# A new head for the first FFN: chunk by chunk, with shift and scale vectors computed as columns

## The chip, the cores and the metric

The kernel runs on one NeuronCore of a Trainium2 chip, in one launch. The metric is the device time of that launch in microseconds. Five engines work side by side, each through its own queue of instructions in order: TensorE (PE in the profile), VectorE (DVE), ScalarE (ACT), GpSimd (POOL) and SyncE (SP), which here issues nearly all DMAs. They wait for each other through semaphores. Weights stream from HBM into SBUF, PE multiplies into PSUM banks, and ACT, DVE and POOL work on what lies between.

## The reference, cut to what matters

Two layers over 256 tokens of width 1024, float32. Every layer is FFN, mixer, FFN; each of the three begins with an RMSNorm whose result is scaled and shifted by vectors that come from one condition vector c:

```python
cond = jax.nn.silu(c)                                  # c: (1, 1024)
for l in range(2):
    mod = cond @ ada_w[l] + ada_b[l]                   # ada_w[l]: (1024, 9 * 1024)
    (sh1, sc1, g1, sh2, sc2, g2, sh3, sc3, g3) = jnp.split(mod, 9, axis=-1)
    n1 = rmsnorm(h, norm_ffn1[l]) * (1 + sc1[:, None, :]) + sh1[:, None, :]
    h = h + 0.5 * g1[:, None, :] * swiglu(n1, ffn1_w_gu[l], ffn1_w_down[l])   # D_FF = 2816
    n2 = rmsnorm(h, norm_mix[l]) * (1 + sc2[:, None, :]) + sh2[:, None, :]
    h = h + g2[:, None, :] * hybrid_mixer(n2, ...)
    n3 = rmsnorm(h, norm_ffn2[l]) * (1 + sc3[:, None, :]) + sh3[:, None, :]
    h = h + 0.5 * g3[:, None, :] * swiglu(n3, ffn2_w_gu[l], ffn2_w_down[l])
return rmsnorm(h, final_norm)
```

swiglu multiplies by w_gu (1024 x 5632: gate and up halves), takes silu(gate) * up, and multiplies by w_down (2816 x 1024). Each of the nine vectors of a layer costs a product of cond with a 1024 x 1024 matrix, 4 MB of weights that are used once.

## The kernel before

**Operands.** Products keep nearly float32 precision with three passes: every operand is split into a rounded part "hi" and the rest "lo", and hi*hi, hi*lo and lo*hi are added in PSUM. `split` (L229) does it for weights: ACT copies a 128x1024 half of a loaded unit into hi (L236), DVE subtracts it from the raw data into lo (L237). Weights come in the order in which the kernel asks for them, packed by the host into one stream. `load` (L209) takes the next unit, mostly 1 MB (128 partitions x 2048 columns), into one of three "raw" buffers; six hi and six lo buffers follow. A buffer is loaded again when its last reader is done, so the SP queue runs ahead by three units at most.

**An FFN** (`ffn`, L645) has 11 blocks of 256 hidden columns. `get_gu` loads and splits a block's gate and up weights (2 MB); `gu_mm` multiplies with the weights as the stationary operand and the transposed activations `nT` as the moving one: 64 matmuls, 32 of 512 columns and 32 of 256. `gu_act` (L740) takes the result out of PSUM (ACT copies, DVE adds, ACT applies silu), POOL multiplies silu(gate) by up (L748), ACT rounds the product and POOL subtracts for the low part (L750). The down product of a block (`down`, L754) is 24 matmuls of 512 columns; it runs one block behind the gate/up product, and the last two blocks' run at the end, tile by tile. Block 0 is different: it is multiplied by rows (tokens on the output partitions, 512 columns), its product transposed on PE afterwards (`rows_act`).

**Shift, scale and gate vectors of later stages** are computed in jobs beside the FFN and mixer blocks, in the order of ADA_PLAN: beside the first FFN G1, SC2, SH2, SC3, SH3; beside the second FFN of layer 0 G3 and then SC1, SH1, SC2 of layer 1; beside the first FFN of layer 1 SH2, G1, SC3, SH3; gates alone elsewhere. One step (`Ada.step`, L406) loads two 128-row slices of the matrix, and DVE multiplies each by its element of cond and accumulates into a 128x1024 sum (L419, L421). After four steps `finish` (L428) adds over the partitions: for a shift or scale 8 transposes on PE (L445, through L194) and two reductions on DVE (L446), for a gate a product with ones. `Jobs.run` spreads the steps over JOB_PARTS blocks.

**The head** (`lead`, L680) works through the list LEAD. It loads the first scale (SC1) and shift (SH1) as row slices in two column spans, 0 to 767 and 768 to 1023. PE forms SC1 as rank-one products, cond element by element against the rows (L484); DVE accumulates SH1 (L489); `cols` (L491) turns both into columns by small matmuls. x is loaded, normalized and transposed meanwhile. With a span's columns there, ACT and DVE modulate and split (`modulate`, L684) and PE multiplies block 0 by rows. Loads that must not disturb are tied to others by `hold`.

**Order.** The program text gives every instruction a priority; a planner with its own timeline fixes the order of each engine's queue before launch, and `high_priority` lifts what is on a stage's edge (norms, gu_act, residuals). `after` adds an ordering by hand.

## Time and profile before

| | |
|---|---|
| median of the runs | 1102.63 us (3 runs, 1100.06 to 1104.28) |
| the profiled execution | 1099.71 us, its span 1097.9 us |
| PE busy | 1064.1 us, 97% |
| DVE busy | 814.3 us, 74% |
| ACT busy | 622.2 us, 57% |
| POOL busy | 219.1 us, 20% |
| DMA | 255.33 MB, 233 GB/s over the span |

Busy times come from one profiled execution. The profile also cuts the span into stretches of chosen length ("windows") with the busy time of each engine, the granted clock of PE as a share of full speed (PEclk) and the data moved; follows the chain of waits back from the last instruction; and lists single instructions by time (the timeline) or in groups by line and shape. PE's matmuls are pipelined, so their recorded durations overlap; the distance between starts is what a matmul costs in a full stream. On DVE the records of neighbours overlap a little as well. "POOL TENSOR_TENSOR" durations include any wait that happens inside the instruction.

### The profile page before, as it was taken

The numbers are of one execution on the slowest core, as the hardware profiler recorded it, in microseconds if no ns is written. First come the engines' busy times: TensorE is split into PE (matmuls) and PEld (weight loads), VectorE is DVE, ScalarE is ACT, GpSimd is POOL, SyncE is SP. The second block draws the span as 40 slices with busy tenths as digits, with TensorE's granted clock in tenths as the row PEclk, the third lists the DMA queues.
The fourth block names the chain that finished last, engine by engine and source line by source line (L and its number), as shares of the span: only waits on it lengthen the run. The fifth ranks groups of instructions, "written<-read, shape, count | busy, mean of one in ns | idle before, by whom it ended". The sixth has DMA issues, their size and how long they took to land.

```text
span 1097.9 us, 15773 instructions
## 1 busy us (share of the span) xinstructions
PE 1064.1 (97%) x5750; PEld 884.0 (81%) x5750; DVE 814.3 (74%) x1327; ACT 622.2 (57%) x1191; POOL 219.1 (20%) x223
## 2 busy tenths in 40 slices
PE   4999999999999999999999999999999999999997
PEld 1688888878888688888878888887788778888885
DVE  4688887877696687786889877886769757656663
ACT  2655454556766665455556554555676657555561
POOL 2022432411000022222311222231200001222221
PEclk9799999999999999999999999999999999999999
DMA  8878987945355187877848787883536515666551
GB/s 296 298 277 347 338 332 263 344 157 215 109 210 192 42 303 283 292 272 259 296 175 305 280 292 288 299 308 134 204 115 204 177 72 198 234 229 227 208 190 38
DMA packets 39997, 255.33 MB, mean 233 GB/s; under 512 B 4936, under 2 KB 5320, under 8 KB 12016
## 3 DMA queue, kind: packets, MB, share of 16 engines
q1 hardware_dynamic: 39168, 252.61, 63.5%
q0 software_dynamic: 752, 1.71, 0.5%
q8 instruction: 45, 0.74, 0.3%
q14 instruction: 32, 0.26, 0.1%
HBM read 253.24 MB, written 1.07 MB: 232 GB/s over the span
## 4 chain that ended last, share of the span: by engine, by line
PE 90%; ACT 3%; DMA 3%; DVE 2%; issue 1%; POOL 1%; SPq 0%; DVEq 0%; POOLq 0%; ACTq 0%
PE pb L189 49%; PE pa L189 38%; PE pb L194 3%; DMA raw<-in_stream_dram 2%; PE pa L194 1%; DVE acc L421 1%; ACT hi L236 1%; DVE lo L237 1%; DMA h<-in_x_dram 0%; ACT z L527 0%; ACT nT L569 0%; ACT z L569 0%; POOL ss L320 0%; POOL pr L748 0%; ACT qkB L1099 0%
## 5 line engine op out<-in xcount | busy, mean ns | idle before, releaser
L237 DVE TENSOR_TENSOR lo<-raw,hi 128x1024 fp32r<-128x1024 f32 (+3 forms) x314 | 381.0, 1229 | 141.7 <-ACT hi L236 139.8
L189 PE MATMUL pb<-nT,hi 128*128 128x512 f32 x1280 | 451.3, 394 | 0.0
L236 ACT CAST hi<-raw 128x1024 fp32r<-128x1024 f32 (+3 forms) x314 | 318.5, 1036 | 195.2 <-PE pb L189 87.6
L189 PE MATMUL pb<-nT,lo 128*128 128x256 f32 x1280 | 358.4, 282 | 0.0
L189 PEld LDWEIGHTS pb<-nT,hi 128*128 128x128 f32 x1280 | 239.2, 188 | 53.4
L189 PEld LDWEIGHTS pb<-nT,lo 128*128 128x128 f32 x1280 | 240.6, 188 | 3.4
L748 POOL TENSOR_TENSOR pr<-sil,pr 128x256 f32<-128x256 f32 x80 | 91.3, 1141 | 492.2 <-DVE pr L745 414.3
L421 DVE SCALAR_TENSOR_TENSOR acc<-raw,cond,acc 128x1024 f32<-128x1024 f32 x118 | 157.5, 1335 | 26.2 <-DMA raw<-in_stream_dram 23.1
L189 PE MATMUL pa<-hi,chh 128*128 128x512 f32 x336 | 106.8, 393 | 0.9 <-ACT chh L750 0.9
L189 PE MATMUL pa<-lo,chh 128*128 128x512 f32 x336 | 106.4, 391 | 0.0
L189 PE MATMUL pa<-hi,chl 128*128 128x512 f32 x336 | 104.8, 392 | 0.0
L750 POOL TENSOR_TENSOR chl<-pr,chh 128x256 fp32r<-128x256 f32 x80 | 90.8, 1134 | 60.0 <-ACT chh L750 60.0
L189 PE MATMUL pa<-hi,nT 128*128 128x488 f32 (+3 forms) x256 | 72.7, 362 | 2.5 <-ACT nT L597 1.6
L189 PEld LDWEIGHTS pa<-hi,chh 128*128 128x128 f32 x336 | 61.5, 188 | 15.6 <-issue 1.4
L189 PEld LDWEIGHTS pa<-lo,chh 128*128 128x128 f32 x336 | 62.9, 188 | 13.2
L189 PEld LDWEIGHTS pa<-hi,chl 128*128 128x128 f32 x336 | 62.3, 188 | 13.1 <-issue 0.3
L750 ACT CAST chh<-pr 128x256 fp32r<-128x256 f32 x80 | 32.5, 406 | 67.2 <-POOL pr L748 66.6
L189 PE MATMUL pa<-nT,hi 128*128 128x256 f32 x352 | 67.1, 288 | 0.0
L747 ACT ACTIVATE sil<-sil 128x256 f32<-128x256 f32 x80 | 33.6, 420 | 43.9 <-DVE sil L745 43.7
L189 PEld LDWEIGHTS pa<-nT,hi 128*128 128x128 f32 x352 | 54.6, 189 | 3.3 <-issue 3.1
L189 PEld LDWEIGHTS pa<-hi,nT 128*128 128x128 f32 x256 | 46.7, 188 | 9.4 <-ACT nT L597 2.2
L189 PE MATMUL pa<-nT,lo 128*128 128x256 f32 x176 | 49.8, 283 | 0.0
(212 smaller groups left out, 1270.7 us busy)
## 6 DMA issues: line engine op xcount, KB each, us to landing
raw<-in_stream_dram SPq DMA_DIRECT2D x218, 1024.0 KB, 4.9
raw<-in_stream_dram SPq DMA_DIRECT2D x16, 384.0 KB, 5.6
raw<-in_stream_dram SPq DMA_DIRECT2D x4, 976.0 KB, 4.8
raw<-in_stream_dram SPq DMA_DIRECT2D x4, 768.0 KB, 4.2
raw<-in_stream_dram SPq DMA_DIRECT2D x4, 640.0 KB, 4.8
up<-in_stream_dram SPq DMA_DIRECT2D x8, 256.0 KB, 7.9
brev<-scr POOLq DMA_DIRECT2D x3, 512.0 KB, 6.6
h<-in_x_dram SPq DMA_DIRECT2D x2, 512.0 KB, 5.2
```

The lines of the kernel that those rows point to most:

```text
L189: last_pe[0] = nc.tensor.matmul(*a, **k)
L194: last_pe[0] = nc.tensor.transpose(*a, **k)
L236: ia = S.copy(hi[:, :n], src)
L237: iv = V.tensor_sub(lo[:, :n], src, hi[:, :n].bitcast(F32))
L421: iv = V.scalar_tensor_tensor(self.acc, src, cond[:, k:k + 1], self.acc, op0=ALU.mult, op1=ALU.add)
L747: S.activation(sil, sil, AF.Silu)
L748: G.tensor_tensor(pr, sil, pr, op=ALU.mult)
L750: last = [S.copy(ch[0], pr), G.tensor_tensor(ch[1], pr, ch[0].bitcast(F32), op=ALU.subtract)]
```

## The change

The first scale and shift, and all shifts and scales of later stages, are computed as columns: the host packs the transposed matrix (`adT`), so that a slice of 128 output columns lies on the partitions with the 1024 inputs along the free dimension, and one multiply by the broadcast silu(c) (`condb`) with a sum along the free dimension gives 128 elements of the vector. `dot` does it in two ways: on DVE in one multiply-reduce, or as a multiply on POOL followed by a copy with accumulation on ACT. In `lead` the scale goes to DVE and the shift to POOL and ACT; in the jobs the two slices of a step go one each way. PE has no part in a shift or scale any more; gates are computed as before.

`lead` is new. For each 128-column chunk of the model width it loads the scale's and the shift's slice (512 KB each, into the eight "x4" buffers) and one unit with this chunk's weights for the first four blocks (1 MB), modulates the chunk (ACT high part, DVE and POOL low part), and multiplies it by rows into all eight PSUM banks (four blocks, two token tiles), 24 matmuls. After eight chunks the four blocks' products are taken out, transposed and split. x is normalized and transposed once into a buffer that later holds the bias tables. Blocks 4 to 10 follow; the down units of blocks 0 to 10 are spread over them by FIRST_DOWN, and the 20 job steps are spread over these seven blocks. The bias table steps move one block later, the rope tables from the head into block 5, x is loaded right after the small columns, and the gains of the mixer move to another buffer.

```diff
-SPAN = 6
-ACT_SHARE = 3
-LEAD_HOLD = 4
-JOB_PARTS = [10, 11, 10, 9]
...
+LEADB = 4
+JOB_PARTS = [7, 11, 10, 9]
+FIRST_DOWN = {4: [0, 1], 5: [2], 6: [3, 4], 7: [5], 8: [6, 7], 9: [8, 9], 10: [10]}
...
+def ada_cols(l, v, k, nk):
+    return ("adT", v, l, (k, k + nk), None)
+
+
+def lead_unit(name, l, k):
+    return ("kc", name, l, (k, k + 1), [(side * DFF + b * 256, 256) for b in range(LEADB) for side in range(2)])
...
+    if kind == "adT":
+        w = inp["ada_w"][l][:, name * D + ks[0] * P:name * D + ks[1] * P]
+        return w.reshape(D, -1, P).transpose(2, 1, 0).reshape(P, -1)
...
+    condb = cst.tile([P, D], F32, name="condb")
+    SY.dma_start(condb, bass.AP(tensor=crow.tensor, offset=crow.offset, ap=[[0, P], [1, D]]))
...
+    S.activation(condb, condb, AF.Silu)
+    onepb = cst.tile([P, KD], F32, name="onepb")
+    V.tensor_scalar(onepb, colt[:, 8 + DEPTH * 24 + KD:8 + DEPTH * 24 + 2 * KD], 1.0, None, op0=ALU.add)
...
+        first_dma = G.dma_start(oh[0:32, 0:512], onehot)
+        after(first_dma, prior[1])
...
+    def dot(src, dst, split_engines):
+        if split_engines:
+            iv = G.tensor_tensor(src, src, condb, op=ALU.mult)
+            S.activation(src, src, AF.Copy, accum_out=dst)
+            return iv
+        return V.tensor_tensor_reduce(out=src, in0=src, in1=condb, op0=ALU.mult, op1=ALU.add, scale=1.0, scalar=0.0,
+                                      accum_out=dst)
+
...
+            (self.row_step if self.v in (G1, G2, G3) else self.col_step)()
...
+        def col_step(self):
+            i = self.i
+            if i == 0:
+                self.m = wk.tile([P, KD], F32, tag="modc", name=nm("modc"), bufs=8)
+            raw = load(ada_cols(self.l, self.v, 2 * i, 2))
+            for kk in range(2):
+                k = 2 * i + kk
+                iv = dot(raw[:, kk * D:(kk + 1) * D], self.m[:, k:k + 1], kk)
+                if hold:
+                    after(iv, hold[1])
...
-            m = wk.tile([P, KD], F32, tag="modc", name=nm("modc"), bufs=8)
-            for j in range(2):
-                p = psB()
-                for k in range(4):
-                    PE.transpose(p[:, k * P:(k + 1) * P], acc[:, (4 * j + k) * P:(4 * j + k + 1) * P], ident)
-                V.reduce_sum(m[:, 4 * j:4 * j + 4], p.rearrange("p (k q) -> p k q", k=4), axis=mybir.AxisListType.X)
+            m = self.m
...
         def lead():
...
+            m = {}
+            for v in (SC1, SH1):
+                m[v] = mods[0, v] = wk.tile([P, KD], F32, tag="modc", name=nm("modc"), bufs=8)
+            raws = {}
+
+            def fetch(k):
+                raws[k] = [load(ada_cols(0, v, k, 1), "x4") for v in (SC1, SH1)] + [load(lead_unit(wgu, l, k))]
+
+            fetch(0)
+            zT = [biasm[:, 4 * j:4 * j + 4, :] for j in range(2)]
+            for t in range(NT):
+                z = norm_z(t)
+                for j in range(2):
+                    p = psA()
+                    for k in range(4):
+                        PE.transpose(p[:, k * P:(k + 1) * P], z[:, (4 * j + k) * P:(4 * j + k + 1) * P], ident)
+                    pv = p.rearrange("p (k q) -> p k q", k=4)
+                    dst = zT[j][:, :, t * P:(t + 1) * P]
+                    S.copy(dst, pv) if j == 0 else V.tensor_copy(dst, pv)
+            banks = None
+            for k in range(KD):
+                if k:
+                    fetch(k)
+                sc, sh, w = raws[k]
+                col = 8 + DEPTH * 24 + k
+                a, b = m[SC1][:, k:k + 1], m[SH1][:, k:k + 1]
+                dot(sc, a, 0)
+                V.tensor_scalar(a, a, onepb[:, k:k + 1], colt[:, 8 + k:9 + k], op0=ALU.add, op1=ALU.mult)
+                dot(sh, b, 1)
+                V.tensor_add(b, b, colt[:, col:col + 1])
+                src = zT[k // 4][:, k % 4]
+                S.activation(nT[0][:, k], src, AF.Identity, bias=b, scale=a)
+                tmp = three("neg", name=nm("zm"))[:, 0:T]
+                V.tensor_scalar(tmp, src, a, b, op0=ALU.mult, op1=ALU.add)
+                G.tensor_tensor(nT[1][:, k], tmp, nT[0][:, k].bitcast(F32), op=ALU.subtract)
+                ws = split_unit(w, 2048)
+                if banks is None:
+                    banks = [[(psB if i < 2 else psA)() for _ in range(NT)] for i in range(LEADB)]
+                for i in range(LEADB):
                     for t in range(NT):
+                        mm3(banks[i][t], [n[:, k, t * P:(t + 1) * P] for n in nT[:2]], ws[i // 2], slice(None),
+                            (slice(None), slice((i % 2) * 512, (i % 2 + 1) * 512)), k == 0, k == KD - 1)
             with tc.high_priority(offset=HP):
+                for i in range(LEADB):
+                    pr = [row_act(p) for p in banks[i]]
+                    p = psB()
+                    for f in range(2):
+                        for t in range(NT):
+                            PE.transpose(p[:, (2 * f + t) * P:(2 * f + t + 1) * P], pr[t][:, f * P:(f + 1) * P], ident)
+                    for f in range(2):
+                        if i == LEADB - 1:
+                            ch = [wk.tile([P, T], F32R, tag="pT", name=nm("cht"), bufs=PTB) for _ in range(2)]
+                        else:
+                            ch = chunk_tile()
+                        pf = p[:, f * T:(f + 1) * T]
+                        S.copy(ch[0], pf)
+                        V.tensor_sub(ch[1], pf, ch[0].bitcast(F32))
+                        act[2 * i + f] = ch
...
+        if first:
+            lead()
+            open_acc()
+            for b in range(LEADB, NB):
+                now = FIRST_DOWN[b]
+                load_dn(now[0])
+                get_gu(b)
+                if now[0] < NB - SKEW:
+                    down_block(now[0])
+                block(b)
+                for d in now[1:]:
+                    load_dn(d)
+                    if d < NB - SKEW:
+                        down_block(d)
                 jobs.run()
-            if first and b in (2, 4, 7):
-                {2: bias_rows, 4: bias_store, 7: bias_flip}[b]()
-            if first and b == 5:
-                rope_tables()
-            hold.clear()
-            if b == 1:
-                for t in range(NT):
-                    for j in range(2):
-                        acc[t][j] = psA()
-            for bd in ([NB - SKEW - 1] if b == NB - 1 else [b - 1] if 1 <= b < NB - SKEW else []):
-                for f in (2 * bd, 2 * bd + 1):
-                    for t in range(NT):
-                        down(f, t, range(2))
+                if b in (5, 6, 8):
+                    {5: bias_rows, 6: bias_store, 8: bias_flip}[b]()
+                if b == 5:
+                    rope_tables()
...
-        gains = wk.tile([P, 448], F32, tag="gains", name=nm("gains"), bufs=1)
+        gains = wk.tile([P, 512], F32, tag="half", name=nm("gains"), bufs=HB)[:, 0:448]
```

## Rows read from the trace of the kernel before

**Rows 1.** The page's first lines: the span, and PE's busy time, share, instructions.

```profile
span 1097.9 us, 15773 instructions
...
PE 1064.1 (97%) x5750; PEld 884.0 (81%) x5750; DVE 814.3 (74%) x1327; ACT 622.2 (57%) x1191; POOL 219.1 (20%) x223
```

**Rows 2.** Windows: stretch, length, busy us (instructions) by engine, PEclk, DMA share, GB/s.

```profile
0.00:10.00 10.00, 0.32 (x2) 0.32 (x3) 5.47 (x32) 4.56 (x12) 3.37 (x10) 1.00 0.71 240
...
10.00:15.00 5.00, 5.00 (x19) 2.36 (x18) 3.73 (x9) 1.24 (x3) 2.51 (x3) 1.00 1.03 392
...
20.00:30.00 10.00, 6.18 (x20) 2.28 (x20) 2.64 (x3) 0.00 (x0) 0.00 (x0) 0.89 0.93 312
30.00:40.00 10.00, 9.57 (x30) 4.99 (x30) 6.87 (x12) 6.55 (x12) 0.00 (x0) 0.50 1.01 386
...
96.00:214.00 118.00, 118.00 (x637) 100.90 (x636) 100.68 (x114) 59.57 (x97) 38.09 (x31) 1.00 0.88 325
...
108.00:124.00 16.00, 16.00 (x88) 12.98 (x86) 14.92 (x19) 9.05 (x15) 5.68 (x4) 1.00 0.95 334
...
381.00:568.00 187.00, 187.00 (x985) 159.70 (x983) 148.10 (x174) 103.82 (x170) 47.71 (x41) 1.00 0.77 276
```

**Rows 3.** The chain of waits by time: start, us, what it ran over.

```profile
24.52 7.15 DMA raw<-in_stream_dram
...
34.22 21.98 PE pb L189 x88
...
226.25 0.73 POOL pr L748
...
228.28 8.88 PE pa L189 x37
...
471.96 0.87 PE pb L194 x8
...
967.04 11.19 PE pb L189 x64
978.24 5.47 PE pa L189 x24
```

**Rows 4.** Timeline: the first projection matmul.

```profile
42.69 0.51 PE L189 MATMUL pb<-hi,nT 128*128 128x512 f32 x1
```

**Rows 5.** Timeline of DVE: start, us, operation; neighbours in order.

```profile
101.33 2.60 DVE L421 SCALAR_TENSOR_TENSOR acc<-raw,cond,acc 128x1024 f32<-128x1024 f32 x2
...
110.06 0.42 DVE L745 TENSOR_TENSOR pr<-pr,pb 128x256 f32<-128x256 f32 x1
110.40 1.22 DVE L237 TENSOR_TENSOR lo<-raw,hi 128x1024 fp32r<-128x1024 f32 x1
111.53 0.69 DVE L446 TENSOR_REDUCE modc<-pb 128x4 f32<-128x512 f32 x1
...
118.27 2.96 DVE L421 SCALAR_TENSOR_TENSOR acc<-raw,cond,acc 128x1024 f32<-128x1024 f32 x2
...
217.94 2.35 DVE L237 TENSOR_TENSOR xlo<-raw,xhi 128x1024 fp32r<-128x1024 f32 x2
```

**Rows 6.** Groups by line and shape: busy us, mean ns, idle before.

```profile
L236 ACT CAST hi<-raw 128x1024 fp32r<-128x1024 f32 x290 | 298.9, 1051 | 187.2 <-PE pb L189 87.6 <-DMA raw<-in_stream_dram 54.2 <-PE pa L189 39.5
...
L748 POOL TENSOR_TENSOR pr<-sil,pr 128x256 f32<-128x256 f32 x80 | 91.3, 1141 | 492.2 <-DVE pr L745 414.3 <-PE pb L189 38.9 <-PE pa L189 13.7
...
L838 POOL TENSOR_TENSOR iqq<-tab 128x160 f32<-128x160 f32 x4 | 2.1, 526 | 0.3
...
L1040 DVE CUSTOM_DVE_ANT_0 neg<-pb,biasm 128x256 f32<-128x256 f32 x32 | 13.5, 421 | 0.0
...
L1040 DVE CUSTOM_DVE_ANT_0 neg<-pb,biasm 128x128 f32<-128x128 f32 x32 | 9.1, 285 | 11.1 <-PE pb L189 11.0
```

**Rows 7.** Timeline of POOL: one multiply beside DVE's work, one alone.

```profile
118.50 1.65 POOL L748 TENSOR_TENSOR pr<-sil,pr 128x256 f32<-128x256 f32 x1 [4.55 <-ACT sil L747]
...
221.95 0.73 POOL L748 TENSOR_TENSOR pr<-sil,pr 128x256 f32<-128x256 f32 x1 [3.43 <-DVE pr L745]
```

More of the change, by code (lines that the diff above doesn't have):

```diff
@@ L541, in trunk, with norm_z @@
     marks = {}
-    def norm_a(t, pp=None):
-        lead = pp is not None
+    def norm_z(t):
         z = wk.tile([P, D], F32, tag="tok", name=nm("z"))
         r = rstd_of(t, z)
-        pp = pp or [psB() for _ in range(2)]
         for j in range(2):
@@ L553, in norm_a, with turn @@
                 S.activation(z[:, js], h[t][:, js], AF.Copy, scale=r)
-        if t == 0 or lead:
-            turn(z, pp, lead)
+        return z
+    def norm_a(t):
+        z = norm_z(t)
+        pp = [psB() for _ in range(2)]
+        if t == 0:
+            turn(z, pp)
         return z, pp
-    def turn(z, pp, lead, behind=None):
+    def turn(z, pp, behind=None):
         for k in range(KD):
-            b, c = (k // 4, k % 4) if lead else (k % 2, k // 2)
-            last_t[0] = PE.transpose(pp[b][:, c * P:(c + 1) * P], z[:, k * P:(k + 1) * P], ident)
+            last_t[0] = PE.transpose(pp[k % 2][:, k // 2 * P:(k // 2 + 1) * P], z[:, k * P:(k + 1) * P], ident)
             if behind and k < 2:
@@ L719, in lead @@
-            for c in LEAD:
-                if c in "ab":
-                    ws.extend(split_unit(load(gu_unit(wgu, l, 0, "ab".index(c))), 2048))
-                elif c == "x":
-                    for t in range(NT):
-                        SY.dma_start(h[t], x[t * P:(t + 1) * P, :])
-                elif c == "n":
-                    pa = [psA() for _ in range(4)]
-                    early = [norm_a(t, [pa[t], pa[2 + t]]) for t in range(NT)]
-                else:
-                    i = int(c[1])
-                    if c[0] in "CS":
-                        (scale if c[0] == "C" else shift).part(i)
-                    elif c[0] in "ms":
-                        (scale if c[0] == "m" else shift).cols(i)
-                    else:
-                        ia, iv = modulate(i)
@@ L736, in lead @@
-            gu_units_[0] = (ws[0:2], ws[2:4])
-            with tc.high_priority(offset=HP):
-                return [row_act(p) for p in banks], ia, iv, shift.end
+            m = {}
[5 more added lines that the diff above has]
+            fetch(0)
@@ new lines, in block, with load_dn, open_acc, down_block @@
+        def block(b):
+            for f in (2 * b, 2 * b + 1):
+                p = [psB(), psB()]
+                gu_mm(p, f, rows_act if f == 2 else None)
+                with tc.high_priority(offset=HP):
+                    prior[:] = gu_act(p, f)
+        def load_dn(b):
+            dn_units_[b] = split_unit(load(dn_unit(wdn, l, b)), 2048, b >= NB - 2)
+        def open_acc():
+            for t in range(NT):
+                for j in range(2):
+                    acc[t][j] = psA()
+        def down_block(b):
+            for f in (2 * b, 2 * b + 1):
+                for t in range(NT):
+                    down(f, t, range(2))
@@ new lines, in ffn @@
+        if first:
[12 more added lines that the diff above has]
+                        down_block(d)
+                jobs.run()
+                if b in (5, 6, 8):
+                    {5: bias_rows, 6: bias_store, 8: bias_flip}[b]()
+                if b == 5:
+                    rope_tables()
+        else:
+            zp = norm_fns[0]()
+            first_holds()
+            get_gu(0)
+            iav = []
+            pr = [gu_rows(0, lambda m: iav.extend(norm_fns[1](*zp, m))), gu_rows(1, None)]
+            for b in range(NB):
+                if b < 2:
+                    hold[:] = iav
+                get_gu(b)
+                if b == 0:
+                    get_gu(1)
+                else:
+                    block(b)
+                load_dn(b)
+                if b < jobs.parts:
+                    jobs.run()
+                hold.clear()
+                if b == 1:
+                    open_acc()
+                for bd in ([NB - SKEW - 1] if b == NB - 1 else [b - 1] if 1 <= b < NB - SKEW else []):
+                    down_block(bd)
```

168 lines of the change are left out of this document (27 added, 141 removed).

## The prediction

> **What bounds the kernel now.** I read the page first: TensorE (PE) is busy 97% of the span [rows 1], so time goes where PE waits or does extra work. The windows come next [rows 2]: from 96 us on PE's records fill every stretch; the gap is before. The chain of waits says where [rows 3]. Up to 34 us it runs over the transfers of the first shift and scale, and the first projection matmul starts at 42.69 us [rows 4]. Later the chain is PE with a steady period: 11.19 us for a block's 64 gate/up matmuls and 5.47 us for its 24 down matmuls, 16.67 us a block, 183.4 us for 11 blocks. The first FFN ends at 228.28 + 8.88 = 237.2 us. Had PE never waited, it would have begun at 53.8: 42.7 us are lost before the first matmul and 11 after it.
>
> DVE is the next engine: busy 100.7 of 118 us between 96 and 214 (85%), and 14.92 of 16 (93%) at its densest; the queue moves 325 GB/s there [rows 2]. DVE's last weight split of the first FFN ends at 217.94 + 2.35 = 220.3 us [rows 5], 17 us before the FFN does. A head that feeds PE earlier therefore gains only what DVE and the queue can follow.
>
> **The change part by part: the head.** Gone are the rank-one matmuls and column transposes that held the first multiplication until 42.69. New, for each 128-column chunk: two column loads (512 KB each), 1 MB of weights, and 24 matmuls of 512 columns. x, the broadcast c and chunk 0 are 3.7 MB; some 2.4 MB land by 10 us and 392 GB/s follow [rows 2], so chunk 0 is in at 13.3. A cast (1.05 [rows 6]) and a subtraction (1.22 [rows 5]) later PE starts, at 15.7 us. Per chunk the limits are these. PE: 24 matmuls as in the down stage, 5.5 us. Queue: 2.1 MB at 334 to 392 GB/s, 5.3 to 6.3. DVE: a multiply-reduce of 1024 columns, two column operations (0.1 each), a 256-column modulation (0.3), two subtractions spaced 1.13 [rows 5]. The multiply-reduce has rows at 128 and 256 columns, 285 and 421 ns [rows 6]: 1.06 ns a column, 1.24 us for 1024, 1.3 with the read of its accumulator. Together 4.1 us. POOL: a 1024-column multiply and a 256-column subtraction.
>
> **The multiply on POOL decides**, and no row shows one of 1024 columns. POOL takes 526 ns for 160 columns [rows 6] and 0.73 us for 256 when undisturbed [rows 7]: 2.1 ns a column, so 2.4 us; four times 0.73 is 2.9; four times the mean with its waits, 1.14 [rows 6], is 4.6. Moreover POOL and DVE hold each other up. The POOL multiply at 118.50 takes 1.65 us and not 0.73: it ends 0.6 us after the first of the two DVE operations beside it does. That DVE pair takes 2.96 us, an undisturbed one 2.60 [rows 5, 7]. So one 256-column POOL operation costs DVE 0.36 us. For 1024 columns the bounds are 0 (it runs beside DVE's idle time or a DVE operation that reads PSUM, as the undisturbed one does) and 2.9 (all of the scaled operation). Four times 0.36 is 1.5; 2.4 less the fixed 0.37 that did not block is 2.0. I take 1.75, between these two.
>
> The Trainium skill (SBUF — State Buffer, section Who interferes with whom) says that a DVE instruction with two SBUF inputs and a GpSimd one that reads SBUF exclude each other for the whole instruction. The rows agree that they exclude each other, but show 0.36 us of 0.73. By the whole instruction the price would be 2.9 us, and the time that of the slow rival below.
>
> A chunk then costs DVE 4.1 + 1.75 + 0.36 = 6.2 us, above PE's 5.5; with some slack 6.7. The lead ends at 15.7 + 7 x 6.7 + 5.5 = 68 us with four blocks of gate/up done, 44.8 us of PE work. Before, PE stood there at 53.8 + 44.8 = 98.6 by the same count: PE is 30 us ahead. DVE is not.
>
> **The first FFN to its end.** DVE's own work up to the last weight split, at back-to-back spacing: lead 8 x 4.1 = 32.5; norm and copies 3; row products and their splits 16 x 0.34 = 5.4; gate/up splits of blocks 4 to 10, 28 x 1.13 = 31.6; down splits 22 x 1.13 = 24.9; PSUM additions 24 x 0.34 = 8.2; gate G1, 8 accumulations x 1.26 and a split, 11.2; 13 multiply-reduces and their small operations, 17.9 (16 in all, 3 fall beside the last block); the rope tables, some 20 small operations that move from the idle head into block 5, and the bias flip, 5.6. Sum 140. What POOL takes from it: 21 multiplies x 1.75 + 32 small ones x 0.36 = 48, of which I hide a quarter (DVE's idle and PSUM time): 36. Total 176 us. At a duty of 90%, between the two above, that is 196 us from the first column at 10 us: 206, against 220.3 now, 14.2 earlier. The last three column steps stand beside the last block: the POOL operations between its last gate/up matmul and the final down matmuls, 0.73 us on the chain [rows 3] and one like it, may each wait behind a multiply: 4 us lost. Net **-10.2**; the FFN ends near 227. PE alone would allow 15.7 + 183.4 + 5 = 204.
>
> ACT gains 1.2 us per POOL column (a pass of the cast's length and a read of the accumulator); it is busy 59.6 of 118 us [rows 2], which hides it. The bias tables' DMAs, moved on POOL's queue behind a product, and the gains' load, moved on SP's queue, have 20 us or more until the mixer reads them: nothing, or at most one POOL operation.
>
> **The two FFNs with shift and scale jobs** (second of layer 0, first of layer 1). Each finish puts 8 transposes on the chain, 0.87 us [rows 3]. Three per FFN go: 2 x 3 x 0.87 = **-5.2**. A vector cost DVE 8 x 1.26 and two reductions of some 0.6, 11 us; now 4 x 1.3 + 0.3 + 4 x 1.75 = 12.5, with DVE busy 148 of 187 us [rows 2], which covers it; without that cover it would be 4.5 us an FFN. The mixers and the last FFN have no shift or scale and stay.
>
> Sum: -10.2 - 5.2 = -15.4 us on the profiled execution's 1099.7 (span 1097.9 and 1.8 around it): 1084.3. The median of the runs shown is 2.9 above that execution, so the forecast is **1087**.
>
> **Rivals.** *PE and the queue bind, the exclusion hides.* For it: PE stays full with DVE at 85%. After the lead at 68, 138.6 us of PE work, 2 of transposes and 3 of the last chain give 212. The queue carries 7 vectors x 4.2 + 33 units x 1.05 + 1.9 = 65.9 MB, 3.1 of them behind the last weights: at 334 GB/s these land at 190, and a split, block 10, the last down matmuls and the chain (29 us) make 219; at 350 it is 211. I take 214: 23 + 5.2 earlier, 1074. Against: 48 us of new exclusion find little idle time.
> *The chunk's chain binds.* If on POOL the next multiply stands behind this chunk's subtraction, a chunk takes 2.4 (multiply) + 1.2 (ACT's sum) + 0.16 + 0.42 (modulation) + 0.73, some 0.35 of handovers, and two waits of 1.1 for a running DVE operation: 7.5 us and not 6.7, 6 us over the lead, 1093. The granted clock adds to it: it fell between 20 and 30 us, when PE was busy 6.2 of 10, and was 0.5 all through 30 to 40 [rows 2]; a lead that leaves PE as thin would run a chunk in 11 us, and two such chunks make 1102. Centre 1098: no change.
> *Slower: the exclusion costs the whole multiply.* At 2.9 us the 21 multiplies cost DVE 21 x 1.15 x 0.75 = 18 more, 20 at 90% duty, and 2 more in the tail; the first FFN ends at 249. The other two still hide it. +12 - 5.2 = +7: 1109. It decides from about 2.6 us per multiply. Should POOL need the 4.6 us of the mean, it is worse.
> That the first blocks do not start early I leave out: their data are the queue's first 4 MB.
>
> **How the numbers follow.** Forecast 0.49 (its own range 1080 to 1096), fast 0.18, chain 0.17, slow 0.16. What a measurement can tell from no change is 0.5%, 5.5 us: 1097.1 to 1108.1. Faster: 0.45 of the forecast, 0.17 of the fast case, 0.06 of the chain, 0.68. Same: 0.03, 0.01, 0.09, and 0.04 of the slow case, 0.17. Slower: the rest, 0.15. The range takes in the fast case and about half of the slow one: 1070 to 1108.
>
> **What would show it.** The first projection matmul at 15 to 17 us; chunks 6.5 to 7 us apart, the lead's last matmul at 64 to 72; POOL's 1024-column multiply at 2.4 us alone and 3.5 behind a DVE operation; DVE busy near 90% up to 206; the first FFN's last down matmul near 227; the second FFN of layer 0 2.6 us shorter. Wrong if the multiply takes over 4 us, chunks are over 7.5 us apart, the granted clock is 0.5 in the lead, or DVE idles while PE is full (then the fast case).

## The result, and the profile after

The changed kernel takes **1139.59 us** against 1101.35 for the kernel before, measured beside it: a ratio of 1.0344, 95% interval [1.0317, 1.037]. The 1139.59 is the median of four runs, one of them disturbed (3439.63 us); the other three, 1136.31 to 1142.12, from which the ratio is taken, have a median of 1137.06. The kernel is 36 to 38 us slower, where 1087 was forecast. The forecast was wrong in its sign.

The page of the changed kernel, first lines (answers to [rows 1]):

```profile
span 1140.4 us, 15556 instructions
...
PE 1060.3 (93%) x5554; PEld 874.6 (77%) x5554; DVE 846.8 (74%) x1314; ACT 661.8 (58%) x1265; POOL 343.3 (30%) x267
```

POOL went from 219.1 to 343.3 us. PE has 196 instructions fewer, and the span is 42.5 us longer. The windows, mostly in the stretches of [rows 2], then in the second FFN of layer 0 (columns as there):

```profile
10.00:20.00 10.00, 3.71 (x13) 3.08 (x14) 7.11 (x11) 4.86 (x8) 5.18 (x3) 0.76 1.02 419
20.00:30.00 10.00, 8.84 (x33) 6.47 (x31) 9.96 (x9) 6.27 (x9) 8.06 (x4) 0.90 1.02 413
30.00:40.00 10.00, 8.66 (x31) 6.90 (x32) 9.82 (x14) 1.79 (x4) 4.99 (x3) 0.83 1.02 415
96.00:214.00 118.00, 108.39 (x530) 89.93 (x529) 95.01 (x113) 61.90 (x106) 69.13 (x41) 0.96 0.79 287
390.60:595.50 204.90, 193.77 (x978) 160.17 (x979) 159.61 (x181) 118.77 (x207) 81.78 (x56) 0.99 0.69 252
```

From 96 to 214 us PE runs 530 matmuls where it ran 637, and its records no longer fill the stretch (how much of that belongs to the multiplies on POOL, the experiments must say). No other engine fills it either: DVE shows 95.0 of 118 (100.7 before), the queue 287 GB/s (325 before). In the second FFN of layer 0 no engine reaches 95% of the 204.9 us. So no engine's total explains the time; the waits between them must. Nor does the granted clock in the second FFN: at 0.99 of 204.9 us it can cost 2.0 us at most. In the first FFN it is 0.96 from 96 to 214 us and 0.82 from there to the end, where PE is busy 29.1 of 37.7 us; what it costs there was not parted from the waits.

Stage by stage. A stage ends here where DVE's last multiplication of its output by the gate starts, ahead of the residual sum; lengths in us, from the profiled executions (1142.12 us the changed kernel's, 1099.71 the other's); "multiplies" are POOL's of 1024 columns in the changed kernel.

| stage | before | after | difference | multiplies |
|---|---|---|---|---|
| first FFN, layer 0 (with the head) | 237.2 | 251.7 | +14.5 | 8 in the head, 16 in jobs |
| mixer, layer 0 | 138.9 | 138.9 | 0 | 0 |
| second FFN, layer 0 | 192.0 | 204.9 | +12.9 | 12 |
| first FFN, layer 1 | 191.8 | 206.4 | +14.6 | 12 |
| mixer and second FFN, layer 1 | 330.7 | 330.6 | -0.1 | 0 |

Exactly the stages with POOL multiplies lost. The head did start earlier: the first projection matmul is at 18.12 us, 42.69 before [rows 4].

```profile
18.12 1.22 PE L196 MATMUL pb<-hi,nT 128*128 128x512 f32 x2 [5.99 <-ACT nT L690]
```

PE's lead over the kernel before is gone by the end of the first FFN, and more.

**One multiply, seen from three engines.** First DVE's timeline (start, us, operation). It shows two head chunks, a rope operation twice and a weight split of the second FFN:

```profile
51.21 4.42 DVE L244 TENSOR_TENSOR lo<-raw,hi 128x1024 fp32r<-128x1024 f32 x2 [1.08 <-ACT hi L243]
55.55 1.21 DVE L419 CUSTOM_DVE_ANT_0 up<-up,condb 128x1024 f32<-128x1024 f32 x1
...
58.76 4.41 DVE L244 TENSOR_TENSOR lo<-raw,hi 128x1024 fp32r<-128x1024 f32 x2 [1.09 <-ACT hi L243]
...
126.25 2.39 DVE L366 SCALAR_TENSOR_TENSOR rt_a<-rt_k,rt_a 128x32 f32<-128x32 f32 x1
...
130.30 0.18 DVE L366 SCALAR_TENSOR_TENSOR rt_a<-rt_k,rt_a 128x32 f32<-128x32 f32 x1
...
445.63 1.23 DVE L244 TENSOR_TENSOR lo<-raw,hi 128x1024 fp32r<-128x1024 f32 x1 [0.57 <-ACT hi L243]
446.77 1.22 DVE L419 CUSTOM_DVE_ANT_0 raw<-raw,condb 128x1024 f32<-128x1024 f32 x1
...
447.91 3.42 DVE L244 TENSOR_TENSOR lo<-raw,hi 128x1024 fp32r<-128x1024 f32 x1
451.25 0.41 DVE L723 TENSOR_TENSOR sil<-sil,pb 128x256 f32<-128x256 f32 x1
```

POOL beside it:

```profile
51.02 2.40 POOL L416 TENSOR_TENSOR up<-up,condb 128x1024 f32<-128x1024 f32 x1
...
58.56 2.39 POOL L416 TENSOR_TENSOR up<-up,condb 128x1024 f32<-128x1024 f32 x1
...
126.13 2.45 POOL L416 TENSOR_TENSOR raw<-raw,condb 128x1024 f32<-128x1024 f32 x1 [0.99 <-DMA raw<-in_stream_dram]
...
446.84 3.41 POOL L416 TENSOR_TENSOR raw<-raw,condb 128x1024 f32<-128x1024 f32 x1 [2.87 <-DMA raw<-in_stream_dram]
```

And ACT:

```profile
446.12 1.05 ACT L243 CAST hi<-raw 128x1024 fp32r<-128x1024 f32 x1 [0.52 <-PE pb L196]
447.07 0.36 ACT L722 COPY sil<-pb 128x256 f32<-128x256 f32 x1
450.28 1.06 ACT L417 ACTIVATE raw<-raw 128x1024 f32<-128x1024 f32 x1 [2.84 <-POOL raw L416]
451.24 0.18 ACT L417 ACTIVATION_READ_ACCUMULATOR raw<-raw 128x1 f32 x1
451.33 1.03 ACT L243 CAST hi<-raw 128x1024 fp32r<-128x1024 f32 x1
```

The two take turns. POOL's multiply of 446.84 lasts 3.41 us instead of 2.40: it waits while DVE's product runs. DVE's split at 447.91 lasts 3.42 us instead of 1.22: it waits until POOL ends at 450.25. DVE loses **2.20 us**, nearly all of POOL's 2.40. A rope operation of 32 columns that takes 0.18 us alone (at 130.30) lasts 2.39 from 126.25 on, with POOL's multiply from 126.13. And ACT stands 2.84 us for POOL's product at a sum of 1.06, while the next weight cast, which needs neither, stands behind that sum until 451.33.

The groups by line and shape (busy us, mean ns, idle before):

```profile
L244 DVE TENSOR_TENSOR lo<-raw,hi 128x1024 fp32r<-128x1024 f32 x290 | 393.8, 1375 | 142.8 <-ACT hi L243 141.9
L416 POOL TENSOR_TENSOR raw<-raw,condb 128x1024 f32<-128x1024 f32 x40 | 120.8, 3022 | 81.6 <-DMA raw<-in_stream_dram 45.8 <-DVE pr L655 14.2 <-DVE xlo L244 7.1
L419 DVE CUSTOM_DVE_ANT_0 raw<-raw,condb 128x1024 f32<-128x1024 f32 x40 | 85.4, 2136 | 15.2 <-DMA raw<-in_stream_dram 15.0
L417 ACT ACTIVATE raw<-raw 128x1024 f32<-128x1024 f32 x40 | 42.5, 1061 | 73.1 <-POOL raw L416 73.1
```

DVE's own product, 1.22 alone, has a mean of 2.14: the other half of the same load arrives with it, so POOL's multiply starts at the same moment. ACT waits 73 us for POOL in all.

### The profile page after: what moved, and what is told of

Same layout as the page of the kernel before. It is cut to its first block, busy times and chain, and to the rows that moved or that the text cites. A ratio compares the mean times of both kernels' runs of the same rounds, so it can differ in the third digit from the quotient of the medians.

```text
span 1140.4 us, 15556 instructions
## 1 busy us (share of the span) xinstructions
PE 1060.3 (93%) x5554; PEld 874.6 (77%) x5554; DVE 846.8 (74%) x1314; ACT 661.8 (58%) x1265; POOL 343.3 (30%) x267
## 3 DMA queue, kind: packets, MB, share of 16 engines
HBM read 253.76 MB, written 1.07 MB: 223 GB/s over the span
## 4 chain that ended last, share of the span: by engine, by line
PE 55%; DMA 12%; DVE 11%; issue 8%; ACT 7%; POOL 6%; SPq 0%; DVEq 0%; POOLq 0%; ACTq 0%
PE pa L196 29%; PE pb L196 24%; DMA raw<-in_stream_dram 11%; DVE lo L244 6%; ACT hi L243 3%; POOL raw L416 3%; PE pb L201 2%; POOL pr L726 2%; ACT raw L417 1%; DVE up L419 1%; PE pa L201 1%; DMA up<-in_stream_dram 1%; POOL chl L728 1%; DVE pr L723 1%; DVE acc L442 0%
## 5 line engine op out<-in xcount | busy, mean ns | idle before, releaser
L244 DVE TENSOR_TENSOR lo<-raw,hi 128x1024 fp32r<-128x1024 f32 (+3 forms) x314 | 417.0, 1345 | 163.8 <-ACT hi L243 162.6
L196 PE MATMUL pb<-nT,hi 128*128 128x512 f32 x1184 | 422.7, 398 | 11.2 <-ACT hi L243 11.2
L196 PE MATMUL pb<-nT,lo 128*128 128x256 f32 x1184 | 334.7, 285 | 5.9 <-DVE lo L244 5.8
L726 POOL TENSOR_TENSOR pr<-sil,pr 128x256 f32<-128x256 f32 x74 | 73.2, 990 | 303.2 <-DVE pr L723 198.5
L416 POOL TENSOR_TENSOR raw<-raw,condb 128x1024 f32<-128x1024 f32 x40 | 120.8, 3022 | 81.6 <-DMA raw<-in_stream_dram 45.8
L419 DVE CUSTOM_DVE_ANT_0 raw<-raw,condb 128x1024 f32<-128x1024 f32 x40 | 85.4, 2136 | 15.2 <-DMA raw<-in_stream_dram 15.0
L196 PE MATMUL pa<-hi,nT 128*128 128x512 f32 (+3 forms) x320 | 94.1, 374 | 2.5 <-ACT nT L572 1.6
L417 ACT ACTIVATE raw<-raw 128x1024 f32<-128x1024 f32 x40 | 42.5, 1061 | 73.1 <-POOL raw L416 73.1
L196 PEld LDWEIGHTS pa<-hi,chh 128*128 128x128 f32 x328 | 60.9, 193 | 25.3 <-ACT hi L243 11.1
L442 DVE SCALAR_TENSOR_TENSOR acc<-raw,cond,acc 128x1024 f32<-128x1024 f32 x48 | 63.3, 1318 | 15.6 <-DMA raw<-in_stream_dram 15.4
L196 PEld LDWEIGHTS pa<-lo,chh 128*128 128x128 f32 x328 | 62.7, 192 | 14.5 <-DVE lo L244 1.1
L196 PEld LDWEIGHTS pa<-hi,nT 128*128 128x128 f32 x320 | 59.6, 192 | 13.0 <-ACT nT L572 2.2
L196 PE MATMUL pb<-hi,nT 128*128 128x512 f32 x160 | 53.3, 415 | 12.3 <-ACT nT L690 6.0
```

Source lines behind the costliest of these rows:

```text
L196: last_pe[0] = nc.tensor.matmul(*a, **k)
L244: iv = V.tensor_sub(lo[:, :n], src, hi[:, :n].bitcast(F32))
L416: iv = G.tensor_tensor(src, src, condb, op=ALU.mult)
L417: S.activation(src, src, AF.Copy, accum_out=dst)
L419: return V.tensor_tensor_reduce(out=src, in0=src, in1=condb, op0=ALU.mult, op1=ALU.add, scale=1.0, scalar=0.0, accum_out=dst)
L442: iv = V.scalar_tensor_tensor(self.acc, raw[:, kk * D:(kk + 1) * D], cond[:, k:k + 1], self.acc, op0=ALU.mult, op1=ALU.add)
```

## The experiments

Two theories. **A, the path over POOL**: each POOL multiply shuts DVE out for its length, and ACT, and the load's buffer, wait behind it. **B**: the columns themselves, the new head or the planner's order cost the time. All times are medians, with the ratio to the kernel before, measured beside them (1100.4 to 1101.8 us). Stage lengths are from one profiled execution of each kernel. The planner lays out every kernel's order anew, so differences of a stage below some 2 us are not read. Diffs are cut to the lines that matter ("...").

**e1_jobs_dve**: the jobs' second product moves from POOL and ACT to DVE; the head stays.

```
-                iv = dot(raw[:, kk * D:(kk + 1) * D], self.m[:, k:k + 1], kk)
+                iv = dot(raw[:, kk * D:(kk + 1) * D], self.m[:, k:k + 1], 0)
```

> The changed kernel, but the second slice of each column job goes to DVE's multiply-reduce like the first; no POOL multiply and no ACT sum beside the FFN blocks, the head unchanged. All theories that put the loss on the POOL/ACT path of the jobs expect the second FFN of layer 0 and the first of layer 1 at about 183 us each (185.8 and 185.9 before, less 2.6 of transposes; 198.8 and 200.8 with the change), the first FFN ending near 238 instead of 252, and a time near 1098. If the loss were in the loads' new order or the new buffers, the two FFNs would stay above 195.

1097.09 us, ratio 0.9969 [0.9953, 0.9984]. First FFN 240.6, second FFN of layer 0 189.2, first of layer 1 190.1. The jobs' 40 POOL multiplies, with ACT's sums behind them, cost 42.5 us (41 by the two ratios).

**e2_all_dve**: the head's second product on DVE as well.

```
-                dot(sh, b, 1)
+                dot(sh, b, 0)
```

> As the run with the jobs on DVE, and the head's shift columns on DVE too. A chunk then costs DVE 4.1 + 1.3 + 0.4 = 5.8 us and has no wait for ACT's sum: chunks 5.8 to 6.2 us apart instead of 7.5, the lead's last matmul near 66 instead of 77, the first FFN ending near 228, and a time near 1087. If the chunk is held by something else (the transfers, the modulation's chain), chunks stay over 7 us apart and the time near 1098.

1088.72 us, ratio 0.9893 [0.9853, 0.9933]: faster than both kernels. First FFN 231.2, so the head's eight multiplies cost 9.4 us there, by this pair of kernels. In its chain of waits the head's later chunks now run on PE without a gap:

```profile
48.87 1.86 PE pb L196 x8
50.73 1.86 PE pa L196 x8
52.59 0.94 PE pb L196 x4
53.52 0.92 PE pa L196 x4
54.44 1.86 PE pb L196 x8
```

24 matmuls in 5.57 us from chunk to chunk; in the changed kernel 7.55 (51.21 to 58.76 above), in which DVE's pair of splits takes 4.42, where an undisturbed pair takes 2.36. With e1 and e2, theory B's columns and head are cleared of the loss. So is the planner's order: each kernel has an order of its own, and of all the runs of this section those without the jobs' POOL multiplies take 1087.9 to 1105.1 us, those with them 1125.9 or more.

One reading of the windows above needs a control. In the stretch from 96 to 214 us e2 has

```profile
96.00:214.00 118.00, 110.15 (x547) 90.61 (x546) 100.91 (x152) 52.48 (x85) 29.27 (x28) 0.97 0.86 324
```

DVE and the queue are back at their values of before, but PE runs 547 matmuls and not 637, and its records don't fill the stretch either. Most of PE's change there comes with the new head and the order behind it. The rest asks what in the POOL path costs how much.

**e3_ghost**: e1, and after each second product on DVE, POOL multiplies the constant row by itself into a spare tile. Nobody waits for it. It adds work that is not used.

```
+                if kk:
+                    ghost = wk.tile([P, D], F32, tag="tok", name=nm("ghost"))
+                    after(G.tensor_tensor(ghost, condb, condb, op=ALU.mult), iv)
```

> The jobs' products all on DVE, and beside each second one POOL multiplies the broadcast vector by itself into a scratch tile that nobody reads: the POOL load and its exclusion with DVE are kept, but no load buffer waits for POOL or ACT. Theory exclusion (DVE blocked for some 2.2 us by each POOL multiply, POOL's products late): the two later FFNs stay at 195 us or more and the time at 1125 to 1145. Theory buffers (a column unit holds one of three load buffers until POOL and ACT are done, and the load queue falls behind): the two FFNs fall to 183 to 187, the time to 1098 to 1105.

1125.85 us, ratio 1.0221 [1.0185, 1.0256]. The FFNs: 256.1, 194.5, 196.8. A multiply that nobody waits for costs 28.8 us against e1, but in the two later FFNs only 5.3 and 6.7, where the changed kernel lost some 16 each. In the first FFN it costs more than the changed kernel's path (256.1 against 251.7), as DVE keeps both products here. So the 28.8 are not simply a part of the 42.5.

**e4_own_buf**: POOL and ACT kept; layer 1's job columns are loaded one by one into other buffers, with a job part's length changed to fit.

```
-JOB_PARTS = [7, 11, 10, 9]
+JOB_PARTS = [7, 9, 9, 9]
...
+                src = raw[:, kk * D:(kk + 1) * D] if raw is not None else load(ada_cols(self.l, self.v, k, 1), "x4")
```

> The changed kernel, with the POOL/ACT path kept, but the columns of layer 1's vectors (all jobs of the second FFN of layer 0 and the first of layer 1) are loaded into the eight separate 512 KB buffers instead of the three that the weights use; these jobs are spread over 9 blocks instead of 11 and 10. Theory buffers: the two FFNs at 183 to 188 us each and the time near 1142 - 26 = 1115. Theory exclusion: they stay at 195 to 201 and the time at 1135 to 1145.

1174.07 us, ratio 1.066 [1.0618, 1.0702]: all expectations missed. The planner moved six of the multiplies forward into the mixer of layer 0 (155.0 us instead of 138.9). The run is confounded and says nothing about the buffers.

**e5_dve_act**: DVE multiplies, ACT still sums; no POOL in the jobs.

```
-            iv = G.tensor_tensor(src, src, condb, op=ALU.mult)
+            iv = (G if split_engines == 1 else V).tensor_tensor(src, src, condb, op=ALU.mult)
...
-                iv = dot(raw[:, kk * D:(kk + 1) * D], self.m[:, k:k + 1], kk)
+                iv = dot(raw[:, kk * D:(kk + 1) * D], self.m[:, k:k + 1], 2 * kk)
```

> The jobs' second product goes to DVE as a plain multiply, and ACT still sums it; POOL has no part in the jobs, the head is left as changed. DVE's work is that of e1_jobs_dve, ACT's is the changed kernel's. Theory A (the harm is POOL's multiply: DVE shut out, and what waits for POOL): first FFN about 241 us, second FFN of layer 0 189 to 191, first of layer 1 190 to 192, whole 1097 to 1101. Rival B (ACT's 1.06 us sums, 37 of them, push its casts back by themselves): second FFN of layer 0 at least 197, whole 1112 or more.

1105.07 us, ratio 1.0025 [1.0002, 1.0048]; FFNs 244.3, 190.3, 193.3. ACT's sums by themselves cost 8 us against e1 (6 by the two ratios), more than A's 0 to 4 and well below B's 15.

**e6_no_sum**: POOL's multiply kept in the jobs, ACT's sum of it left out.

```
-            S.activation(src, src, AF.Copy, accum_out=dst)
+            if split_engines == 1:
+                S.activation(src, src, AF.Copy, accum_out=dst)
...
-                iv = dot(raw[:, kk * D:(kk + 1) * D], self.m[:, k:k + 1], kk)
+                iv = dot(raw[:, kk * D:(kk + 1) * D], self.m[:, k:k + 1], 2 * kk)
```

> POOL's multiply stays in the jobs, but ACT's sum of its product is left out (so half of the jobs' shift and scale columns are zero in this run). Theory A1 (exclusion alone, no chain behind POOL): second FFN of layer 0 near e3_ghost's 194.5 us, first FFN of layer 1 near 196.8, whole about 1115 to 1123. Theory A2 (ACT's queue stands still at a sum that waits for POOL, and the casts behind it come late): the same numbers here, the 10 us to the changed kernel's 204.9 and 206.4 being the sum's. Rival C (POOL, late and slow, holds the load's buffer and with it the next transfer, whatever ACT does): second FFN of layer 0 at 202 us or more, first of layer 1 at 203 or more, whole above 1130.

1131.9 us, ratio 1.0253 [1.0218, 1.0288]; FFNs 252.5, 198.1, 198.8. The two FFNs lie between both expectations, the whole where rival C had it. Against e1 this is +11.9, +8.9 and +8.7 us for 16, 12 and 12 multiplies: **0.73 to 0.74 us each**, in all three stages, net of the product that DVE no longer makes. ACT's sum behind POOL adds 6.8 and 7.6 us in the later FFNs, and nothing in the first (251.7 with it). That these 7 us are ACT's queue standing is read from the waits; the sum also holds the load's buffer a little longer, and no run parts the two. By e5 the sum's own work makes 1.1 and 3.2 of them. In the second FFN of layer 0 the waits of the changed kernel (total us, times, longest) have

```profile
DVE lo L244 <- ACT hi L243: 29.4, 28, 2.9
ACT raw L417 <- POOL raw L416: 29.3, 11, 5.2
POOL raw L416 <- DMA raw<-in_stream_dram: 18.0, 9, 2.9
```

and those of e1 in the same stage

```profile
ACT hi L243 <- PE pb L196: 28.5, 21, 3.3
...
ACT hi L243 <- PE pa L196: 12.8, 12, 1.4
```

In e1 ACT's casts wait for PE to free their targets: the weights are ahead of PE. In the changed kernel such waits are no longer among the nine longest; ACT waits for POOL instead, and PE waits for casts and splits:

```profile
PE pb L196 <- ACT hi L243: 4.7, 5, 1.2
PE pb L196 <- DVE lo L244: 3.2, 4, 0.8
```

In e1 PE waits for neither in this stage.

**e10_ghost_raw**: e3 with the spare multiply reading the job's load.

```
-                    after(G.tensor_tensor(ghost, condb, condb, op=ALU.mult), iv)
+                    after(G.tensor_tensor(ghost, raw[:, D:2 * D], condb, op=ALU.mult), iv)
```

> As e3_ghost, but POOL's spare multiply reads the job's load instead of the constant row, so that it holds the load's buffer until POOL is done, as it does in e6_no_sum; its product still goes nowhere. Theory (the buffer held by POOL is what e6_no_sum has beyond e3_ghost in the two later FFNs): second FFN of layer 0 at 198 us or more, first of layer 1 at 199 or more, whole 1130 or more. Rival (no matter who holds the buffer; e6_no_sum's difference is the place of the multiply in the order): 194 to 195.5 and 196 to 198, whole 1122 to 1128.

1153.47 us, ratio 1.0486 [1.0459, 1.0513]; FFNs 266.5, 201.7, 204.8: 7.2 and 8.0 us more than e3 in the later two, though POOL multiplies as often and as much. The waits of the load queue (SP's) in the second FFN show it:

```profile
SPq L225 <- DVE lo L244: 89.7, 18, 15.3
SPq L225 <- POOL ghost L457: 40.5, 11, 6.3
```

The next transfer waits for POOL to let go of the buffer; in e3 no such wait is listed. So a held buffer costs time, which e4 could not test. How much of it is in the changed kernel is not shown. Here POOL's multiply waits for DVE's product first (49.3 us in this stage), so the buffer is held longer than in e6 or in the changed kernel, and e10 loses more than either in the first FFN. For a job's load SP waits 18.1 us in e1, 51.3 in e6 (44.6 for DVE's product, 6.7 for POOL's) and 25.2 in the changed kernel (18.4 for DVE's product, 6.8 for ACT's sum).

**e11_pieces**: each POOL multiply cut into four of 256 columns.

```
-            iv = G.tensor_tensor(src, src, condb, op=ALU.mult)
+            for c in range(0, D, 256):
+                iv = G.tensor_tensor(src[:, c:c + 256], src[:, c:c + 256], condb[:, c:c + 256], op=ALU.mult)
```

> The changed kernel, but each POOL multiply of 1024 columns is cut into four of 256. Theory (DVE is shut out for the length of a POOL operation, whatever its size): DVE loses at least as much in sum, but one operation of it no more than about 0.7 us at once, and POOL is busy longer (0.73 us a piece, 2.9 in sum against 2.4): whole 1135 to 1150. Rival (the length of one hold does the harm, as it delays one cast by 2.2 us): whole 1115 to 1130, second FFN of layer 0 below 200.

1150.64 us, ratio 1.0449 [1.0417, 1.0481], second FFN of layer 0 207.5; just past the theory's end, and the rival is out. Shorter holds don't help:

```profile
L417 POOL TENSOR_TENSOR raw<-raw,condb 128x256 f32<-128x256 f32 x160 | 166.8, 1074 | 83.8 <-DMA raw<-in_stream_dram 38.2 <-DVE xlo L244 15.4 <-DVE pr L656 14.4
L420 DVE CUSTOM_DVE_ANT_0 raw<-raw,condb 128x1024 f32<-128x1024 f32 x40 | 61.0, 1525 | 26.4 <-DMA raw<-in_stream_dram 25.0 <-POOL raw L417 1.0
L418 ACT ACTIVATE raw<-raw 128x1024 f32<-128x1024 f32 x40 | 42.4, 1060 | 89.6 <-POOL raw L417 89.6
```

A piece takes POOL 1.07 us in the mean, beside DVE, and 0.73 alone [rows 7]. The chain from the load over POOL to ACT becomes longer: 166.8 us by 40 products is 4.2 each, instead of 3.0. But the theory came near by another way than its own: it had DVE lose at least as much, and DVE loses less. Its own product has a mean of 1.53 us instead of 2.14, its busy time is 799.0 us instead of 846.8, and the kernel is 11 us slower all the same. What grew is POOL's time and ACT's wait for it, 89.6 us instead of 73.1. So the time that DVE loses is not by itself what the kernel loses.

**Where e2's gain comes from.** e8_row_jobs keeps the new head on DVE and makes the jobs' shifts and scales as rows, as before. e9_old_head is the kernel before with only the jobs' columns, on DVE.

```
-            (self.row_step if self.v in (G1, G2, G3) else self.col_step)()
+            self.row_step()
...
```

The rest of e8's edit brings the row sums, transposes and reductions back; e9's is the change's own column code, put into the kernel before, and is not shown.

> The new head with all its dots on DVE, but the jobs make their shifts and scales as rows, as before the change (accumulate 1024 wide rows, turn them with eight transposes and a reduction). It splits e2_all_dve's gain over the kernel before into head and column jobs. Theory (the eight transposes, the reduction and their wait go with the rows, 2 to 3 us an FFN): second FFN of layer 0 about 192 us, first of layer 1 about 191.8, first FFN 231 to 234, whole 1093 to 1097. Rival (those FFNs differ because of the order the planner chose, not because of columns): 189 to 190 and 190, whole 1088 to 1090.

> The kernel before with its own head, in which only the jobs' shifts and scales are made as columns, every dot on DVE (the broadcast row that the dots need is loaded behind the head). e8_row_jobs, with the new head and rows, took as long as before; so: theory (e2_all_dve's gain is all the columns', the head's is nothing): first FFN 229 to 234 us, second FFN of layer 0 about 189.2, first of layer 1 about 190, whole 1087 to 1092. Rival (the columns help only beside the new head, whose jobs are squeezed into seven of eleven blocks): first FFN 236 to 238, whole 1094 to 1098.

e8: 1104.07 us, ratio 1.0009 [0.9988, 1.0031]; FFNs 238.3, 191.8, 191.7. e9: 1101.37 us, ratio 1.0000 [0.9982, 1.0018]; FFNs 242.0, 189.3, 190.1. Columns shorten the two later FFNs by 2.7 and 1.7 us whatever the head; the missing transposes, which the prediction had at 2.6 each, would explain it. In the first FFN neither half gains alone (238.3 and 242.0 against 237.2), both together do (231.2): both of the expectations for that stage missed. Why was not settled; each kernel has another planned order there. So a split of the first FFN's loss into parts, from pairs of kernels, is uncertain by some 5 us.

**e7_rope_early**: e2 with the rope tables ahead of the head.

```
+            rope_tables()
             lead()
...
-                if b == 5:
-                    rope_tables()
```

> All dots on DVE as in e2_all_dve, and the rope tables are worked out before the head's loop instead of behind block 5. Theory A (the tables' small operations stood in the way of DVE's casts in the first FFN, while the head's first 15 us leave DVE and POOL idle): first FFN 225 to 229 us against 231.2, whole 1081 to 1086. Rival (the first FFN is bound elsewhere after its head, by transfers or the PE): 230 to 232, whole 1087 to 1089. If the tables delay the first projection matmul behind 19 us, the whole is 1090 or more.

1091.17 us, ratio 0.9882 [0.9845, 0.992]; first FFN 232.0, mixer 141.5. Nothing gained: the rival was right on the first FFN, and in e2 the tables' small operations are not what it waits for. The whole is 2 us past the rival's end; the mixer is 2.6 us longer than in e2, and the first projection matmul, at 17.11 us, is not late.

**e12_no_pool**: e2, and POOL's 156 operations of 256 columns in the FFNs on DVE too.

```
-                G.tensor_tensor(nT[1][:, k], tmp, nT[0][:, k].bitcast(F32), op=ALU.subtract)
+                V.tensor_tensor(nT[1][:, k], tmp, nT[0][:, k].bitcast(F32), op=ALU.subtract)
...
-            G.tensor_tensor(pr, sil, pr, op=ALU.mult)
+            V.tensor_tensor(pr, sil, pr, op=ALU.mult)
...
-            last = [S.copy(ch[0], pr), G.tensor_tensor(ch[1], pr, ch[0].bitcast(F32), op=ALU.subtract)]
+            last = [S.copy(ch[0], pr), V.tensor_tensor(ch[1], pr, ch[0].bitcast(F32), op=ALU.subtract)]
```

> e2_all_dve with the 256-column operations of POOL in the FFNs (the product and the low part behind each gate/up pair, 74 each, and the eight subtractions of the head) on DVE as well. POOL takes 0.73 us for one, DVE 0.33 by back-to-back spacing. Theory (what a POOL operation shuts DVE out for is at least what DVE needs for the work itself, at 256 columns too): DVE has no more to do than before, 156 x 0.33 = 51 us more work against 156 holds of 0.36 to 0.7 us less, and the chain behind a pair is shorter; chunks of the head 5.0 to 5.6 us apart against 5.7, first FFN 223 to 230 us against 231.2, whole 1078 to 1087. Rival (the small operations fall beside DVE's idle time or its reads of PSUM, where POOL is free): DVE gains 20 to 50 us of work in all, first FFN 233 to 240, whole 1090 to 1100.

1087.9 us, ratio 0.9876 [0.9856, 0.9895], as e2. First FFN 226.4, 4.8 us shorter as expected, but the two mixers are 142.6 and 143.1 (138.9 and 141.3 in e2). The first window of this kernel's first mixer has PE at a granted clock of 0.83, where e2's has 1.00; whether that is cause or follows from PE's idle time was not tested. The windows of the second FFN, this kernel's and then e2's:

```profile
371.00:559.00 188.00, 187.19 (x975) 159.18 (x975) 157.32 (x243) 105.86 (x179) 2.62 (x4) 1.00 0.74 274
```

```profile
371.00:559.00 188.00, 186.76 (x972) 159.07 (x971) 147.90 (x203) 106.64 (x181) 45.50 (x44) 1.00 0.75 274
```

DVE has 40 operations and 9.4 us more there. By 0.33 us each they are 13.2, so by this estimate the 40 holds had cost it 3.8, 0.1 us each: the theory's sentence that they cost DVE as much as the work itself is wrong at 256 columns.

## Why the prediction was wrong

**Right.** POOL's multiply alone: forecast 2.4 us, measured 2.40. DVE's product with its read: forecast 1.3, measured 1.22 and 0.08. The columns' saving in the two later FFNs, 5.2 us in the forecast, is 4.5 (e1 against before). A chunk bound by PE at 5.5 us shows in e2, 5.57.

**Step 1 that failed: "I take 1.75, between these two".** The price of one multiply to DVE is 2.20 us, next to the whole operation. Both of its scalings, 1.5 and 2.0, start from a 256-column operation that hid half of itself [rows 5, 7]; what hides at 0.73 us does not at 2.4, when DVE has its next operation waiting. e11 bears this out: beside four short pieces DVE's product has a mean of 1.53 us, beside one long multiply 2.14. The lower bound was misread as well: the undisturbed multiply at 221.95 does not run beside a read of PSUM, as DVE's last one (221.44, 0.42 us) has ended; it runs beside DVE's idle time. The sentence set beside it was the better one: the Trainium skill (SBUF — State Buffer, section Who interferes with whom) has the two engines exclude each other for the whole instruction, and the trace agrees, 3.42 us against 1.22. The slow rival rested on this. Its 249 us for the first FFN came near the measured 251.7, but by a price of 2.9, more than the 2.4 that the prediction itself gave POOL's whole multiply, and with nothing for ACT's queue or the buffer: that is luck. The point from which it was to decide, 2.6, was too high.

**Step 2 that failed: "of which I hide a quarter", and DVE's duty of 90%.** The sum treated exclusion as more work for DVE, to be packed into its idle time. DVE's record from 96 to 214 us is 81% full (95.0 of 118), its holds included, and the stage is late all the same. What is lost is order, as far as the waits show it. Both products come from one load, so POOL's multiply starts as DVE's does, DVE's splits wait, PE's weights come late, and the queue idles (287 GB/s, 324 in e2). The first FFN was forecast 10.2 us shorter and came out 14.5 longer: 9.4 are the head's eight multiplies (e2 to e1), 11.1 the sixteen in its jobs (e1 to the changed kernel), and without both it is 6.0 shorter (each uncertain by some 5 us, as e8 and e9 show). That last number is short of the sum too: with the 21 products on DVE its terms give 140 + 21 x 1.3 + 9 = 176 us as before, so 10 to 14 us gained. In e2 DVE is busy 100.9 and PE 110.2 of the 118 us from 96 to 214; what PE lacks there was not settled.

**Step 3 that failed, and the largest: "DVE busy 148 of 187 us [rows 2], which covers it"** for the two later FFNs. Forecast -5.2, measured +27.5 us: 32.7 of the 57.4 us by which the stages of the profiled execution missed (the first FFN has the other 24.7). The sum named the price without that cover, 4.5 us an FFN; that was too low as well. By e6 POOL's multiply costs 0.74 us each, 8.9 and 8.7 us; ACT's sum behind it adds 6.8 and 7.6; the columns give back 2.8 and 1.7. These add up to +12.9 and +14.6, the measured differences, as they must: each term is the difference between two neighbouring kernels. The share of busy time said that DVE has time for it in the mean. It did not say that DVE's, POOL's and ACT's in-order queues and a load buffer would each stand for the multiply.

**Step 4 that failed: "it is busy 59.6 of 118 us [rows 2], which hides it".** "It" is ACT, and it had the time for 1.2 us a column. But an in-order engine pays for the wait as well: 73 us in all for POOL, with casts behind it. For POOL's own queue the prediction did ask what stands behind a multiply; for ACT's sum that question was not put. Without POOL the same sums cost 6 to 8 us in the whole (e5).

**The head.** The first matmul was forecast at 15.7 us and came at 18.12. Chunk 0 was to be in at 13.3; its weights land at 14.5, though its shift slice is there at 12.0. The rest is the column's way over POOL and ACT, which starts its first cast only at 15.59; in e2, with the weights at 15.1, the matmul comes at 16.96. Chunks were 7.55 us apart, not 6.7. The chunk's rival had that number, 7.5, and a falling clock; the clock fell to 0.76 and 0.83, not to 0.5 [rows 2]. It priced the chain at 6 us over the lead, where e1 to e2 is 9.4: not the main loss.

## What to carry to other kernels

Before work is moved from DVE to POOL, set POOL's duration, not DVE's, against the DVE time that it frees: here 2.2 us were taken from DVE to free 1.2, and putting the work back on DVE made a kernel slower by 3.4% into one faster by 1.1%. A busy share below 100% covers an addition only if nothing that PE needs stands behind it in an in-order queue, and only if the operand's buffer comes free as soon as before; so list, for each added wait, what is behind it. When a small operation's cost is scaled up to a long one, scale the whole duration, as what hid the small one is used up.

## What the runs showed of the hardware that was not expected

An operation of DVE on 32 columns, 0.2 us alone, lasts 2.39 beside a POOL multiply: the hold goes by POOL's length, not by the size of what it meets. POOL in turn waits for DVE: four pieces of 256 columns take 1.07 us each beside DVE and 0.73 alone, so cutting a long operation took time off DVE's record (799.0 us busy instead of 846.8) and put more on POOL's (405.8 instead of 343.3), and the kernel lost more. At 256 columns most of the hold is hidden in this kernel, by estimate about 0.1 us each of 0.73 (e12).
